# A decoder layer on one core: the recurrence's gates from exact parts, 1/rms moved into evictions, larger first transfers, and a last product in one piece

## The chip, the cores and the metric

The kernel runs on one core of a Trainium2 chip. A core has engines with queues of their own: TensorE (PE, matrix products; its weight loads are PEld), VectorE (DVE), ScalarE (ACT), GpSimd (POOL) and SyncE (SP), which here issues nearly all transfers. The metric is the device time of one execution in microseconds. One more execution is recorded by the hardware profiler, and the profile and the trace come from that one.

## The reference

The reference is one layer of a hybrid decoder in float32, for 256 tokens of 2048 features. What matters here:

```python
hn = rmsnorm(h, norm_mix_w)
q, k, v, g_ret, xr, yr, g_a, g_b = split(hn @ w_in)
q, k = rotary(q), rotary(k) * RET_QK_DIM ** -0.5
ret_out = silu(g_ret) * head_groupnorm(chunkwise_retention(q, k, v))
xr = causal_dwconv(xr, rnn_conv_w, rnn_conv_b)           # 4 taps
# rg_lru: block-diagonal gates, 16 blocks of 128 features
gate_r = sigmoid(einsum("bsgi,gij->bsgj", xb, w_a) + b_a)
gate_i = sigmoid(einsum("bsgi,gij->bsgj", xb, w_x) + b_x)
a = exp(-8 * gate_r * softplus(-lam))
u = sqrt(1 - a * a) * (gate_i * xr)
hr = scan(h_t = a_t * h_{t-1} + u_t)
merged = sigmoid(g_a) * (ret_out @ w_proj_ret) + sigmoid(g_b) * ((gelu(yr) * hr) @ w_proj_rnn)
h = h + merged @ w_mix_out
# then cross-attention over 256 memory tokens, a gated FFN (2 x 5632) with a
# 3-tap convolution, and a last rmsnorm
```

## The kernel before

**Products of exact parts.** Each float32 matrix is split into `hi`, its value rounded to the type float32r, and `lo`, the rest, so that hi + lo is exact. A large product is the sum of three products of such parts, h·hi, l·hi and h·lo (`products_n`, L314). For weights, ACT makes `hi` (L278; for the very first chunk DVE, L276) and DVE makes `lo` (L279). For the left operands `split_pair` (L394) and `split_cols` (L420) do the same. The small products inside the recurrence, `rgw` times `xr`, are the exception: they are plain float32 matmuls (L711).

**The weight stream.** All weights lie in one array, `wall`, in the order of use. A chunk is 4 k-tiles of 128 rows by 512 columns, 1 MB, that is 8 KB for each partition, and makes 24 products (2 token halves × 4 k-tiles × 3). `prefetch` (L232) loads a chunk into `raw` (3 buffers), and splits it into `hi` and `lo` (6 buffers each, two k-tiles in one), two chunks ahead of the products. `chunks` (L291) hands it to the GEMM. The first two GEMMs, q and v, are interleaved and start with smaller pieces: the first two chunks have 2 k-tiles each, and come in transfers of 2 KB for a partition; the next four in transfers of 4 KB. The left operand x, transposed (`xt`), comes two k-tiles at a time (`Pairs`, L489), in step with the weights.

**The order.** A matmul is kept in program order (`mm`, L212). The other engines' order is set by a scheduler, which takes instructions by program order and readiness; `tc.high_priority(300)` moves some ahead. `later(n, fn)` (L287) puts the call of `fn` behind the end of the chunk n+1 chunks on. So the code between GEMMs is spread over the chunks that follow. SP issues the transfers in its order, and one that waits holds up those behind it.

**1/rms of the tokens.** The first norm's weight is folded into the split of x; the factor 1/rms (`rs0`) is per token and is only known after 39 us, when x has been loaded a second time in rows and its squares summed on ACT (`sum_squares`, L462). For q and k it is put into the tables: `spread_tokens` (L447) makes two diagonal tiles of `rs0` on DVE, and PE multiplies them with ones, which spreads `rs0` over the partitions (`rsb`); `tables` (L538) multiplies sin and cos by it. For all other outputs it goes into the eviction.

**From rows to features.** A GEMM leaves tokens on partitions. `turned_rows` (L383) copies the accumulator to `rows` on DVE with high priority (L389, or L391 with the factor), ACT separates 16-bit planes (L367), two DMA transposes turn them, and one or more chunks later ACT joins them into `f` (L378), features on partitions.

**The recurrence.** It runs in four blocks b of 512 features (L735). GEMM XR of the block is turned; `conv_x` (L741) makes `xr` with ACT (L746) and DVE (L748). `RG_WAIT` = 3 chunks (and one) after that, `recur` (L704) does two of the four gate tiles at a time (`pr` = 0, 1): four float32 matmuls, eight activations on ACT (L713 to L716), and products on DVE. After the second pair follow a square root (L728), which needs another activation table, and the scan on DVE (L731), which writes to `xr`. GEMM YR of the block goes to `gelu_y` (L763), 4 chunks after it for b < 3 and 3 chunks for b = 3; it ends in two `rnn` tiles, gelu(yr) times the scan, split into parts (L401, L402). The tiles of block b are the left operand of the chunk b of w_proj_rnn (L798): `gated` (L782) runs a GEMM with O_GB first, 4 chunks, and then w_proj_rnn, 4 chunks. So block 3's tiles are needed first in the fourth chunk of the first w_proj_rnn GEMM.

**The end.** The last 512 columns of ffn_w_down (12 k-tiles here) are done by `last_down` (L986): first token half and then the second, each in two pieces of 256 columns, so that the addition of the residual and the sum of squares of one piece run under the products of the next. Each piece has an accumulator tile; `accs[0]` holds columns 0 to 255 of both token halves, `accs[1]` the others.

Tiles of 4 KB a partition come from one pool, `big`, with 27 buffers; small PSUM tiles (`sm`) have 2 buffers and accumulators (`acc`, two token halves × 512) 3.

Of the kernel before, what the change touches and what calls it, by code (L numbers as in the profile page):

```python
# [17 lines left out]
P = 128  # L18
# [17 lines left out]
FREE = 300  # L36
RG_WAIT = 3
EPS = 1e-6
# [6 lines left out]

C_ID, C_INVF, C_SIGN, C_DEC = 0, 128, 129, 130
C_WIDTH = 130 + HEADS * S


def constants():  # L50
    c = np.zeros((P, C_WIDTH), np.float32)
    c[:, C_ID : C_ID + P] = np.eye(P, dtype=np.float32)
# [85 lines left out]
def hybrid_layer(  # L138
# [45 lines left out]
    def load_rows(src, c, cs=slice(0, BW), t=None):  # L184
# [5 lines left out]
        return t  # L190

    NF2 = 2 * NF
    pa = cp.tile([P, P], F32, name="pa")
# [3 lines left out]
    cid = cp.tile([P, C_DEC], F32, name="cid")  # L197
    ident = cid[:, C_ID : C_ID + P]
    invf = cid[:, C_INVF : C_INVF + 1]
# [22 lines left out]
    def load_x(n):  # L222
        while len(xin) < n:
            t = big([P, 2, BW], s="nat")
            rows = x[0].rearrange("(t p) d -> p t d", p=P)
            c = len(xin) * BW
            sp.dma_start(out=t, in_=rows[:, :, c : c + BW])
            xin.append(t)

    at = [0]  # L230

    def prefetch(n):  # L232
        while len(ahead) < n and taken[0] < len(stream):
# [12 lines left out]
            own = early and i % 2 == 0  # L246
            cuts = range(nk + 1) if i < 2 else range(0, nk + 1, KH) if i < 6 else (0, nk)
            if own:
                xs.load(k2 + 1)
            for a, b in zip(cuts, cuts[1:]):  # L250
                sp.dma_start(out=raw[:, a:b, :], in_=src[:, a:b, :])  # L251
                if i == 0 and a == 0:
                    sp.dma_start(out=xs.rest[0], in_=xs.rest[1])  # L253
                elif own and a == 0:
                    xs.load(k2 + nk // KH)
            if i >= 6:
                load_x(min(4, 2 * i - 11))
            if i == 8:
                sp.dma_start(out=cid, in_=consts[:, 0:C_DEC])
                sp.dma_start(out=pa[:, 16:P], in_=by_feature[:, 16:P])  # L260
                sp.dma_start(out=pb, in_=by_feature[:, P : P + 80])
            if i == 13:
                sp.dma_start(out=pf.rearrange("p a n -> p (a n)"), in_=by_feature[:, P + 80 :])
            if i in (8, 9):
                for b in (2 * i - 16, 2 * i - 15):
                    sum_squares(xin[b], ss0, b, pin=True)
            parts = []
# [114 lines left out]

    def turned_rows(a, r, then, wait=1):  # L383

        rows = big([P, 2, BW], s="rows")
        with tc.high_priority(FREE):
            for tt in range(2):
                if r is None:
                    dve.tensor_copy(rows[:, tt, :], a[:, tt, :])  # L389
# [54 lines left out]

    rsb = cp.tile([P, S], F32, name="rsb")

    def spread_tokens(r):  # L447

        diag = tp.tile([P, S], F32, tag="tr", bufs=2, name=nm("diag"))
        for tt in range(2):  # L450
            dve.tensor_scalar_mul(diag[:, tt * P : (tt + 1) * P], ident, r[:, tt : tt + 1])

        def products():
            bc = small((P, S))
            for tt in range(2):
                cs = slice(tt * P, (tt + 1) * P)
                mm(bc[:, cs], ones, diag[:, cs], start=True, stop=True)
            act.copy(rsb, bc)

        return products  # L460

    def sum_squares(rows, ss, c, pin=False):  # L462

        for tt in range(2):
            junk = tp.tile([P, BW], F32, tag="tmp", name=nm("junk"))
            i = act.activation(junk, rows[:, tt, :], AF.Square, accum_out=ss[:, tt, c : c + 1])
            if pin:
                tc.keep_in_program_order(i)

# [8 lines left out]

    ss0 = sums()

# [8 lines left out]
    class Pairs(list):  # L489
# [3 lines left out]
        def load(self, n):  # L493

            while len(self.raw) < n:
                k2 = len(self.raw)
                t = tmp("xt")
                src = self.src[:, 2 * k2 : 2 * k2 + 2, :]
                if k2 == 0 and self is xs:
                    sp.dma_start(out=t[:, 0, :], in_=src[:, 0, :])  # L500
                    self.rest = (t[:, 1, :], src[:, 1, :])
                else:
                    sp.dma_start(out=t, in_=src)  # L503
                self.raw.append(t)

# [14 lines left out]
    posi = big([P, S], I32, s="posi")  # L520
    sp.dma_start(out=posi, in_=positions[0].partition_broadcast(P))

    rs0 = rstd_rows(ss0)
    spread0 = spread_tokens(rs0)
    dve.tensor_scalar_mul(half_rs0, rs0, 0.5)
# [12 lines left out]
    def tables():  # L538
        spread0()
        ang, turns, red = (tmp("rot")[:, 0, :] for _ in range(3))  # L540
# [7 lines left out]
        dve.tensor_scalar(out=red, in0=red, scalar1=3.1415925, scalar2=-3.1415925, op0=ALU.min, op1=ALU.max)  # L548
        act.activation(sin, red, AF.Sin)
        dve.scalar_tensor_tensor(out=ang, in0=red, scalar=-1.0, in1=red, op0=ALU.mult, op1=ALU.max)  # L550
        dve.tensor_scalar(out=ang, in0=ang, scalar1=-1.0, scalar2=float(np.pi / 2), op0=ALU.mult, op1=ALU.add)
        act.activation(cos, ang, AF.Sin)
        dve.scalar_tensor_tensor(out=sin, in0=sin, scalar=sign, in1=rsb, op0=ALU.mult, op1=ALU.mult)
        dve.tensor_tensor(out=cos, in0=cos, in1=rsb, op=ALU.mult)

# [147 lines left out]

    def recur(b, rgw, xr, pr, aa, tt_, ti):  # L704

        for j in (2 * pr, 2 * pr + 1):
# [28 lines left out]
    for b in range(4):  # L735
        rgw = big([P, 2, 4, P], s="rgw")
        for i, src in enumerate((rg_w_a, rg_w_x)):
            sp.dma_start(out=rgw[:, i], in_=src[0, 4 * b : 4 * b + 4].rearrange("g i j -> i g j"))
        xr = {}

        def conv_x(f, b=b, xr=xr, rgw=rgw):  # L741
            xr[0] = big([P, 4, S], s="xr")
# [9 lines left out]

            three = []

            def both(pr):
                if pr == 0:
                    three.extend(big([P, 4, S], s=n) for n in ("aa", "tt", "ti"))
                recur(b, rgw, xr[0], pr, *three)

# [47 lines left out]
    hrow = [load_rows(x, c) for c in range(4)]  # L807
    mnat = [load_rows(mem, c) for c in range(4)]
    ms = Pairs(mem_t, p_mem, 3)
# [35 lines left out]
    def memory_steps(b):  # L845
        if b == 0:
            ss = sums()
            for c in range(4):
# [137 lines left out]
    def last_down(b0, hid, n, b):  # L986
# [4 lines left out]
        accs = [acc(), acc()]  # L991
        parts = [p for _, _, ps in chunks(n, "ffn_w_down", b0 * BW, b * BW) for p in ps]
        for tt in range(2):
            last = big([P, BW + 1], s="last")
            before = sp_.tile([P, 1], F32, tag="pt3", bufs=2, name=nm("pt3"))
            for c in range(2):
                cs = slice(c * S, (c + 1) * S)
                for k in range(n):
                    hi, lo = (t[:, k % KH, cs] for t in parts[k // KH])
                    for _ in products_n(accs[c][:, tt, 0:S], hid[k // 2][:, k % 2, :], hi, lo, tt, k == 0, k == n - 1):  # L1000
                        pass
                y = last[:, c * S : (c + 1) * S + c]
                dve.tensor_add(last[:, cs], h[:, tt, cs], accs[c][:, tt, 0:S])
                junk = tp.tile([P, S + 1], F32, tag="tr", bufs=2, name=nm("junk"))
# [85 lines left out]
```

## Time and profile before

| what | value |
|---|---|
| median of 3 runs | 2006.91 us (2006.58 to 2007.68) |
| the profiled execution's own time | 2007.17 us |
| its span | 2005.4 us |
| mean granted TensorE clock | 0.999 |
| PE busy | 1995.0 us, 9012 records |
| DVE / ACT busy | 1264.9 / 1257.4 us |
| HBM read | 388.46 MB, 195 GB/s over the span |
| groups: L279 lo, DVE, 714 instructions | 859.7 us, mean 1219 ns |
| L278 hi, ACT, 712 instructions | 733.3 us, mean 1048 ns |
| L378 f, ACT, 120 instructions | 158.2 us, mean 1354 ns |
| L391 rows, DVE, 68 instructions | 47.7 us, mean 743 ns |

The span runs from the first to the last instruction; the time of the execution is 1.77 us longer. A group's mean is the duration of one instruction from start to end; where one follows another at once, they start some 0.08 to 0.10 us closer than that. In the views of the trace every row has the start in microseconds from the beginning of the span, the duration (of the whole run, where several alike follow one another), the engine and what it does; what stands in brackets is idle time just before it and what ended that. In the chain of waits each piece starts where the one before it ends. PE's matmul records for a float32 matmul come twice, so x8 there are four matmuls.

### The profile page before, as it was taken

How to read it: one execution, taken by the hardware profiler on the slowest of the kernel's cores; microseconds unless marked ns; L12 is line 12 of the kernel's file. 1: busy time of each engine (PE TensorE's matmuls, PEld its weight loads, DVE VectorE, ACT ScalarE, POOL GpSimd, SP SyncE). 2: the span in 40 equal slices, each digit the busy share in tenths (PEclk: the TensorE clock that was granted, in tenths of full speed). 3: DMA queues.
4: the chain of work that ended last, by engine and by line, in shares of the span. 5: the costliest groups of instructions: out<-in, count | busy, mean ns of one | idle time of the engine just before them, and what ended most of it. 6: DMA issues, size and time to landing. Idle time of an engine off the chain costs nothing.

```text
span 2005.4 us, 23496 instructions
## 1 busy us (share of the span) xinstructions
PE 1995.0 (99%) x9012; PEld 1660.5 (83%) x9012; DVE 1264.9 (63%) x1562; ACT 1257.4 (63%) x1508; POOL 8.8 (0%) x14
## 2 busy tenths in 40 slices
PE   9999999999999999999999999999999999999998
PEld 7888888888888888888888888888888888888887
DVE  6857756888545555466555554667774576754775
ACT  6646647988444555586676655767763577734773
POOL 0000000000000000000000000000000000000000
PEclk9999999999999999999999999999999999999999
DMA  8765757765555656787667546677775577656673
GB/s 305 243 224 164 240 197 210 220 206 184 211 192 192 202 196 215 264 273 219 216 214 215 183 169 196 223 200 230 212 229 190 179 229 221 217 201 202 207 231 126
DMA packets 191488, 423.54 MB, mean 211 GB/s; under 512 B 133776, under 2 KB 138512, under 8 KB 146320
## 3 DMA queue, kind: packets, MB, share of 16 engines
q1 hardware_dynamic: 190944, 421.52, 64.3%
q8 instruction: 70, 1.15, 0.2%
q10 hardware_dynamic: 432, 0.53, 0.1%
q14 instruction: 42, 0.34, 0.0%
HBM read 388.46 MB, written 2.10 MB: 195 GB/s over the span
## 4 chain that ended last, share of the span: by engine, by line
PE 98%; issue 0%; DMA 0%; DVE 0%; SPq 0%; ACT 0%; POOLq 0%; POOL 0%
PE acc L213 96%; PE sm L213 3%; DMA raw<-in_wall 0%; DVE lo L279 0%; SPq L251 0%; ACT nat L1024 0%; DVE rows L389 0%; ACT hi L278 0%; POOLq L1086 0%; POOL last L1012 0%; SPq L503 0%; SPq L253 0%; SPq L500 0%; POOLq L1012 0%
## 5 line engine op out<-in xcount | busy, mean ns | idle before, releaser
L213 PE MATMUL acc<-hi,s 128*128 128x512 f32 (+1 forms) x5744 | 1758.6, 388 | 0.9 <-DVE hi L276 0.9
L213 PEld LDWEIGHTS acc<-hi,s 128*128 128x128 f32 x5744 | 1073.9, 188 | 220.9 <-issue 1.6
L279 DVE TENSOR_TENSOR lo<-raw,hi 128x1024 fp32r<-128x1024 f32 (+1 forms) x714 | 859.7, 1219 | 600.3 <-ACT hi L278 579.9
L213 PE MATMUL acc<-lo,s 128*128 128x512 f32 (+1 forms) x2872 | 1112.1, 387 | 0.7 <-DVE lo L279 0.7
L278 ACT CAST hi<-raw 128x1024 fp32r<-128x1024 f32 (+1 forms) x712 | 733.3, 1048 | 490.7 <-PE acc L213 450.0
L213 PEld LDWEIGHTS acc<-lo,s 128*128 128x128 f32 x2872 | 539.2, 188 | 111.6 <-DVE lo L279 1.6
L378 ACT COPY f<-pt 128x1024 uint16<-128x1024 uint16 x120 | 158.2, 1354 | 94.7 <-DMA pt<-pl 94.7
L367 ACT COPY pl<-rows 128x1024 uint16<-128x1024 uint16 x92 | 91.6, 1043 | 41.8 <-DVE rows L391 37.5
L939 DVE SCALAR_TENSOR_TENSOR fg<-f,pf,fg 128x255 f32<-128x255 f32 (+1 forms) x88 | 37.4, 479 | 29.5 <-ACT fg L937 29.1
L391 DVE TENSOR_SCALAR rows<-acc,ro 128x512 f32<-128x512 f32 x68 | 47.7, 743 | 1.7 <-PE acc L213 1.6
L939 DVE SCALAR_TENSOR_TENSOR fv<-f,pf,fv 128x255 f32<-128x255 f32 (+1 forms) x88 | 36.1, 478 | 4.7 <-ACT fv L937 4.6
L425 DVE SCALAR_TENSOR_TENSOR s<-f,pb,s 128x256 fp32r<-128x256 f32 x48 | 20.1, 479 | 4.9 <-ACT s L424 4.9
L937 ACT ACTIVATE fg<-f,pf 128x256 f32<-128x256 f32 x44 | 22.9, 591 | 0.3
L937 ACT ACTIVATE fv<-f,pf 128x256 f32<-128x256 f32 x44 | 23.1, 591 | 0.0
L748 DVE SCALAR_TENSOR_TENSOR xr<-f,pa,xr 128x255 f32<-128x255 f32 (+2 forms) x48 | 20.2, 476 | 3.2 <-ACT xr L746 3.1
L424 ACT ACTIVATE s<-f,pb 128x256 fp32r<-128x256 f32 x48 | 20.6, 497 | 0.0
L367 ACT COPY pl<-nat 128x1024 uint16<-128x1024 uint16 x16 | 15.9, 1042 | 7.3 <-DVE nat L823 7.3
L213 PEld LDWEIGHTS sm<-s,s 128*128 128x128 f32 x144 | 18.8, 191 | 0.9
L213 PE MATMUL sm<-s,s 128*128 128x256 f32 (+1 forms) x144 | 18.6, 279 | 0.0
L957 ACT ACTIVATE ft<-fg 128x512 f32<-128x512 f32 x22 | 13.8, 629 | 7.3 <-DVE fg L939 7.3
L413 ACT ACTIVATE v<-acc,ro 128x512 fp32r<-128x512 f32 x16 | 10.9, 682 | 10.9 <-DVE v L414 10.9
L401 ACT ACTIVATE s<-fo 128x512 fp32r<-128x512 f32 x22 | 13.6, 633 | 4.1 <-DVE fo L959 4.1
(146 smaller groups left out, 578.1 us busy)
## 6 DMA issues: line engine op xcount, KB each, us to landing
raw<-in_wall SPq DMA_DIRECT2D x352, 1024.0 KB, 4.9
nat<-in_x SPq DMA_DIRECT2D x8, 512.0 KB, 8.3
raw<-in_wall SPq DMA_DIRECT2D x6, 512.0 KB, 8.1
nat<-in_mem SPq DMA_DIRECT2D x4, 512.0 KB, 8.6
xt<-in_mem_t SPq DMA_DIRECT2D x8, 256.0 KB, 5.6
pt<-pl SPq DMA_TRANSPOSE x120, 3.3
xt<-in_x_t SPq DMA_DIRECT2D x7, 256.0 KB, 8.4
out<-nat SPq DMA_DIRECT2D x6, 256.0 KB, 2.9
```

The source lines that it names most:

```text
L213: tc.keep_in_program_order(pe.matmul(*a, **k))
L278: act.copy(hi[:, ds], raw[:, cs, :])
L279: dve.tensor_tensor(out=lo[:, ds], in0=raw[:, cs, :], in1=hi[:, ds].bitcast(F32), op=ALU.subtract)
L367: act.copy(planes[:, tt], words[:, tt])
L378: act.copy(halves_[:, :, :, cs], turned_[:, :, :, cs])
L391: dve.tensor_scalar_mul(rows[:, tt, :], a[:, tt, :], r[:, tt : tt + 1])
L424: act.activation(t[:, j, 0:S], src[:, j, :], AF.Identity, scale=wcol(j))
L425: dve.scalar_tensor_tensor(out=t[:, j, S:BW], in0=src[:, j, :], scalar=wcol(j), in1=t[:, j, 0:S].bitcast(F32), op0=ALU.mult, op1=ALU.subtract,
L748: dve.scalar_tensor_tensor(out=y[:, s:S], in0=z[:, 0 : S - s], scalar=p_cw(3 - s, t), in1=y[:, s:S], op0=ALU.mult, op1=ALU.add,)
L937: act.activation(y, z[:, j, :], AF.Identity, scale=pf[:, 2, t : t + 1], bias=pf[:, 3, t : t + 1])
L939: dve.scalar_tensor_tensor(out=y[:, s:S], in0=z[:, j, 0 : S - s], scalar=pf[:, 2 - s, t : t + 1], in1=y[:, s:S], op0=ALU.mult, op1=ALU.add,)
L957: act.activation(th, gt[:, cs, :], AF.Tanh, scale=0.5)
```

## The change

1. The gates of the recurrence become three products of exact parts (`product`, L350), 256 columns wide, instead of a float32 matmul. `parts_of` makes the parts: `hi` by ACT, `lo` by DVE, as tiles of 128 × 1024 from `big`; for the gate weights 4 chunks after the block's start, for `xr` 2 chunks after `conv_x`. `RG_WAIT` goes from 3 to 4, so that both pairs of gates stand a chunk later.
2. The tables of sin and cos no longer hold 1/rms; `rsb`, `spread_tokens` and the identity in `consts` go. `turned_rows` of q and k multiplies by `rs0` (L391's form); for the first q it is not urgent any more. The sign goes into the activation of sin.
3. The first transfers: the second chunk comes in one piece of 4 KB a partition instead of two of 2 KB; `xt` from the third pair on comes in four k-tiles (4 KB); x and mem for the sums of squares come in half rows (4 KB) with one activation each, in place. The early transfers are kept in program order.
4. In `last_down`, the first token half is one product of 512 columns into `accs[0][:, 0, :]`; the second stays in two pieces, into `accs[0][:, 1, 0:256]` and `accs[1][:, 1, 0:256]`.

```diff
-RG_WAIT = 3
+RG_WAIT = 4
...
+    def load(out, in_, pin):
+        i = sp.dma_start(out=out, in_=in_)
+        if pin:
+            tc.keep_in_program_order(i)
+
+    def load_half(src, i):
+
+        t = big([P, 2 * BW], s="nat")
+        load(t, src[0, i // 2 * P : (i // 2 + 1) * P, i % 2 * 2 * BW : (i % 2 + 1) * 2 * BW], src is x)
+        return t
...
-            cuts = range(nk + 1) if i < 2 else range(0, nk + 1, KH) if i < 6 else (0, nk)
+            cuts = range(nk + 1) if i == 0 else range(0, nk + 1, KH) if i < 6 else (0, nk)
...
-    def turned_rows(a, r, then, wait=1):
+    def turned_rows(a, r, then, wait=1, urgent=True):
         rows = big([P, 2, BW], s="rows")
-        with tc.high_priority(FREE):
+        with tc.high_priority(FREE) if urgent else nullcontext():
...
+    def sum_squares(rows, ss, i):
+
+        tc.keep_in_program_order(act.activation(rows, rows, AF.Square, accum_out=ss[:, i // 2, i % 2 : i % 2 + 1]))
...
-                t = tmp("xt")
-                src = self.src[:, 2 * k2 : 2 * k2 + 2, :]
+                many = 1 if k2 < 2 else 2
+                t = big([P, 2 * many, S], s="xt")
+                src = self.src[:, 2 * k2 : 2 * (k2 + many), :]
...
-        spread0()
...
-        act.activation(sin, red, AF.Sin)
+        act.activation(sin, red, AF.Sin, scale=sign)
...
-        dve.scalar_tensor_tensor(out=sin, in0=sin, scalar=sign, in1=rsb, op0=ALU.mult, op1=ALU.mult)
-        dve.tensor_tensor(out=cos, in0=cos, in1=rsb, op=ALU.mult)
...
-            turned_rows(a, None, rotate_both, 2 - b if g + b else 3)
+            turned_rows(a, rs0, rotate_both, 2 - b if g + b else 3, g + b > 0)
...
+    def parts_of(src):
+
+        hi, lo = (big(list(src.shape), F32R, s="rp") for _ in range(2))
+        act.copy(hi, src)
+        dve.tensor_tensor(out=lo, in0=src, in1=hi.bitcast(F32), op=ALU.subtract)
+        return hi, lo
...
-                mm(gp[:, i, :], rgw[:, i, j, :], xr[:, j, :], start=True, stop=True)
+                product(
+                    gp[:, i, :], [t[:, i, j, :] for t in wparts], [t[:, j, :] for t in xparts], True, True
+                )
...
+        later(3, lambda wparts=wparts, rgw=rgw: wparts.extend(parts_of(rgw)))
...
+            three, xparts = [], []
+            later(1, lambda: xparts.extend(parts_of(xr[0])))
...
+        def total(o, tt, cs):
+            for k in range(n):
+                hi, lo = (t[:, k % KH, cs] for t in parts[k // KH])
+                for _ in products_n(o, hid[k // 2][:, k % 2, :], hi, lo, tt, k == 0, k == n - 1):
+                    pass
...
+            if tt == 0:
+                total(accs[0][:, 0, :], tt, slice(0, BW))
             for c in range(2):
                 cs = slice(c * S, (c + 1) * S)
-                for k in range(n):
-                    hi, lo = (t[:, k % KH, cs] for t in parts[k // KH])
-                    for _ in products_n(accs[c][:, tt, 0:S], hid[k // 2][:, k % 2, :], hi, lo, tt, k == 0, k == n - 1):
-                        pass
+                o = accs[c][:, 1, 0:S] if tt else accs[0][:, 0, cs]
+                if tt:
+                    total(o, tt, cs)
...
-                dve.tensor_add(last[:, cs], h[:, tt, cs], accs[c][:, tt, 0:S])
+                dve.tensor_add(last[:, cs], h[:, tt, cs], o)
```

More of the change, by code (lines that the diff above doesn't have):

```diff
@@ L1 @@
-from contextlib import ExitStack
+from contextlib import ExitStack, nullcontext
 import numpy as np
@@ L44 @@
 O_XR, O_YR, O_GA, O_GB = 6144, 8192, 10240, 12288
-C_ID, C_INVF, C_SIGN, C_DEC = 0, 128, 129, 130
-C_WIDTH = 130 + HEADS * S
+C_INVF, C_SIGN, C_DEC = 0, 1, 2
+C_WIDTH = C_DEC + HEADS * S
 def constants():
     c = np.zeros((P, C_WIDTH), np.float32)
-    c[:, C_ID : C_ID + P] = np.eye(P, dtype=np.float32)
     half = DK // 2
@@ L197, in hybrid_layer @@
     cid = cp.tile([P, C_DEC], F32, name="cid")
-    ident = cid[:, C_ID : C_ID + P]
     invf = cid[:, C_INVF : C_INVF + 1]
@@ L223, in load_x @@
         while len(xin) < n:
[L224 to L228, printed above, removed]
+            xin.append(load_half(x, len(xin)))
     at = [0]
@@ L250, in prefetch @@
             for a, b in zip(cuts, cuts[1:]):
-                sp.dma_start(out=raw[:, a:b, :], in_=src[:, a:b, :])
+                load(raw[:, a:b, :], src[:, a:b, :], early)
                 if i == 0 and a == 0:
-                    sp.dma_start(out=xs.rest[0], in_=xs.rest[1])
+                    load(*xs.rest, early)
                 elif own and a == 0:
@@ L258, in prefetch @@
             if i == 8:
-                sp.dma_start(out=cid, in_=consts[:, 0:C_DEC])
-                sp.dma_start(out=pa[:, 16:P], in_=by_feature[:, 16:P])
-                sp.dma_start(out=pb, in_=by_feature[:, P : P + 80])
+                load(cid, consts[:, 0:C_DEC], True)
+                load(pa[:, 16:P], by_feature[:, 16:P], True)
+                load(pb, by_feature[:, P : P + 80], True)
             if i == 13:
-                sp.dma_start(out=pf.rearrange("p a n -> p (a n)"), in_=by_feature[:, P + 80 :])
+                load(pf.rearrange("p a n -> p (a n)"), by_feature[:, P + 80 :], True)
             if i in (8, 9):
                 for b in (2 * i - 16, 2 * i - 15):
-                    sum_squares(xin[b], ss0, b, pin=True)
+                    sum_squares(xin[b], ss0, b)
             parts = []
@@ L442, in hybrid_layer @@
     p_xa, p_mem, p_ffn = (col(pb, b) for b in (32, 48, 64))
[L445 to L468, printed above, removed]
+    def sum_squares(rows, ss, i):
+        tc.keep_in_program_order(act.activation(rows, rows, AF.Square, accum_out=ss[:, i // 2, i % 2 : i % 2 + 1]))
     def sums():
@@ L477, in rstd_rows @@
         return rsqrt_small(var, 2, 1.0 / D, EPS)
-    ss0 = sums()
+    ss0 = sums()[:, :, 0:2]
     def rsqrt_small(ap, n, scale, eps):
@@ L496, in load @@
                 k2 = len(self.raw)
-                t = tmp("xt")
-                src = self.src[:, 2 * k2 : 2 * k2 + 2, :]
+                many = 1 if k2 < 2 else 2
+                t = big([P, 2 * many, S], s="xt")
+                src = self.src[:, 2 * k2 : 2 * (k2 + many), :]
                 if k2 == 0 and self is xs:
-                    sp.dma_start(out=t[:, 0, :], in_=src[:, 0, :])
+                    load(t[:, 0, :], src[:, 0, :], True)
                     self.rest = (t[:, 1, :], src[:, 1, :])
                 else:
-                    sp.dma_start(out=t, in_=src)
-                self.raw.append(t)
+                    load(t, src, self is xs)
+                self.raw += [t[:, 2 * i : 2 * i + 2, :] for i in range(many)]
         def __getitem__(self, i):
@@ L520, in hybrid_layer @@
     posi = big([P, S], I32, s="posi")
-    sp.dma_start(out=posi, in_=positions[0].partition_broadcast(P))
+    load(posi, positions[0].partition_broadcast(P), True)
     rs0 = rstd_rows(ss0)
-    spread0 = spread_tokens(rs0)
     dve.tensor_scalar_mul(half_rs0, rs0, 0.5)
@@ L702, in hybrid_layer, with recur @@
     rnn = []
-    def recur(b, rgw, xr, pr, aa, tt_, ti):
+    def parts_of(src):
[3 more added lines that the diff above has]
+        return hi, lo
+    def recur(b, wparts, xparts, xr, pr, aa, tt_, ti):
         for j in (2 * pr, 2 * pr + 1):
@@ L738, in hybrid_layer, with conv_x @@
             sp.dma_start(out=rgw[:, i], in_=src[0, 4 * b : 4 * b + 4].rearrange("g i j -> i g j"))
-        xr = {}
-        def conv_x(f, b=b, xr=xr, rgw=rgw):
+        xr, wparts = {}, []
+        later(3, lambda wparts=wparts, rgw=rgw: wparts.extend(parts_of(rgw)))
+        def conv_x(f, b=b, xr=xr, wparts=wparts):
             xr[0] = big([P, 4, S], s="xr")
@@ L751, in conv_x @@
                     )
-            three = []
+            three, xparts = [], []
+            later(1, lambda: xparts.extend(parts_of(xr[0])))
             def both(pr):
@@ L757, in both @@
                     three.extend(big([P, 4, S], s=n) for n in ("aa", "tt", "ti"))
-                recur(b, rgw, xr[0], pr, *three)
+                recur(b, wparts, xparts, xr[0], pr, *three)
             for pr in range(2):
@@ L807, in hybrid_layer @@
     hrow = [load_rows(x, c) for c in range(4)]
-    mnat = [load_rows(mem, c) for c in range(4)]
+    mnat = [load_half(mem, i) for i in range(4)]
     ms = Pairs(mem_t, p_mem, 3)
@@ L846, in memory_steps @@
         if b == 0:
-            ss = sums()
+            ss = sums()[:, :, 0:2]
             for c in range(4):
```

## The prediction

> **What bounds the kernel now.** I read the busy times and the chain of waits first.
>
> ```profile
> PE 1995.0 (99%) x9012; PEld 1660.5 (83%) x9012; DVE 1264.9 (63%) x1562; ACT 1257.4 (63%) x1508; POOL 8.8 (0%) x14
> ...
> PE 98%; issue 0%; DMA 0%; DVE 0%; SPq 0%; ACT 0%; POOLq 0%; POOL 0%
> ```
>
> PE is the chain from 13 us to 1991 us. So a PE microsecond saved is a microsecond of span, and work added on ACT or DVE is free until PE has to wait for it. The pieces of the chain in order of time (start, us, what) give PE's prices:
>
> ```profile
> 4.02 6.79 DMA raw<-in_wall
> 10.81 0.02 issue
> 10.84 1.06 ACT hi L278
> ...
> 45.74 1.29 DVE rows L389 x2
> 47.03 1.14 DVE lo L279
> ...
> 481.25 5.45 PE acc L213 x24
> 486.70 1.73 PE sm L213 x8
> 488.43 484.17 PE acc L213 x2136
> 972.60 2.87 PE sm L213 x24
> 975.48 43.55 PE acc L213 x192
> ```
>
> A product with 512 columns costs 43.55/192 = 0.2268; with 256 columns 2.87/24 = 0.1196; four float32 gate matmuls (8 records) 1.73, so 0.4325 each. A chunk of 24 products lasts 5.45. Outside the head the only breaks in PE are one at 48 and the tail.
>
> Whether ACT and DVE have room is not read from 63% but from the recurrence. Busy time there, two stretches (stretch, length, then PE, PEld, DVE, ACT):
>
> ```profile
> 398.00:425.00 27.00, 27.00 (x121) 22.36 (x120) 25.11 (x36) 26.54 (x32) 0.00 (x0) 1.00 0.65 213
> 480.00:491.00 11.00, 11.00 (x50) 9.23 (x49) 6.15 (x8) 10.96 (x20) 0.00 (x0) 1.00 0.59 232
> ```
>
> ACT is full at the very place where the change gives it more; DVE is at 93% in the first. The clock column is 1.00, so PE's prices hold.
>
> **The change part by part.** The sum is made against the profiled execution, 2007.17 (span 2005.4 and 1.77 around it), 0.26 above the median of 2006.91; the differences are then put on the median.
>
> *Gates on PE.* 32 float32 matmuls go: 32 × 0.4325 = 13.84. 96 products of 256 columns come: 96 × 0.1196 = 11.48. **−2.36**.
>
> *1/rms in the evictions.* The diagonal's two matmuls go (0.36, from 45.54 to 45.91), and with them the wait at 48.22, where PE wants a lo that DVE does after the urgent pair of rows (the 1.29 above). From 45.32 to 48.56 there are 10 products: 3.24 against 10 × 0.2268 = 2.27, so **−0.97**. The rows now need rs0, which POOL finishes at 39.0, well before 45.7. sin and cos lose two DVE multiplies, a product wait nobody has; nothing on the path.
>
> *4 KB pieces.* The head's waits of PE:
>
> ```profile
> 5.24 1.42 PE L213 MATMUL acc<-hi,s 128*128 128x512 f32 x4 [0.41 <-DVE hi L276]
> ...
> 7.59 1.17 PE L213 MATMUL acc<-hi,s 128*128 128x512 f32 x4 [0.48 <-DVE hi L276]
> ...
> 13.20 0.50 PE L213 MATMUL acc<-lo,s 128*128 128x512 f32 x1 [0.53 <-DVE lo L279]
> ```
>
> In all PE loses about 2.0 here (0.98 around 7.6, 0.24 at 11.9, 0.80 at 13.2, with the refill after each). Throughput is about 320 GB/s from 7 to 10 us, where 2 KB pieces land, and about 420 from 10 to 16. The second chunk's raw, 0.52 MB, would save 0.39 us at the better rate, and SP issues one transfer fewer (0.47) ahead of the next. Against that its first casts wait for all 4 KB rather than for 2 KB. I take **−0.3**; bounds −1.0 (both later waits gone) and +0.5 (one cast's length later). In the Trainium skill, DMA: Bandwidth & Descriptors, section "Why small descriptors are slow (HBM only)", joining descriptors is worth it only up to 256 B each; by that, 2 KB to 4 KB gives 0 instead of −0.3. The two rates here speak for a gain, but other transfers are mixed in, and the difference is within my bounds.
>
> *Squares* of x (and mem) now take one activation of 128x1024 a load, about the 1.06 of the square root's row, instead of two of 128x512 of 0.62 each with a read of 0.18: less ACT work before 39 us, off the path. The order of x and xt on SP's queue moves (xt in 4 k-tiles, after the raw it used to precede); PE has no wait between 14 and 45 that this could lengthen by the rows, so 0, held by the ±0.5 above.
>
> *The last piece.* The first tokens' 72 products of 256 columns (17.27/144 = 0.1199 each in that stretch, 8.63) become 36 of 512 (8.16): −0.47. But the two half accumulators become one tile, and the second tokens' first product uses it too: it waits for both additions that read the first tokens' result.
>
> ```profile
> 1984.79 0.42 DVE L1003 TENSOR_TENSOR last<-nat,acc 128x256 f32<-128x256 f32 x1
> ```
>
> PE's last product ends 0.39 after issue; then two additions (0.42 and 0.34 in line), with 0.04 to pass each semaphore: about 1.2 less the 0.23 that PE would have spent anyway, 1.0 to 1.1. Net **+0.6**; if the wait isn't there, −0.47.
>
> *ACT and DVE in the recurrence, where I see the loss.* Per block of 512 features come two splits into parts (of the gate weights and of xr): on ACT 2 casts of 128x1024 like L278's (1.05), on DVE 2 subtractions like L279's (1.22), so 8.4 and 9.8 us in all. And the gates stand a chunk later. I went along the changed program's queues with the durations of the rows above, letting each instruction start when its engine and its operands are ready; the same walk on the old program gives PE one wait in this kernel's middle, 0.37 at 45, as the trace has it (0.39).
>
> Block 3 decides. Its rnn tiles are the left operand of w_proj_rnn's fourth chunk. Before, after the second pair of gates:
>
> ```profile
> 488.14 0.48 ACT L713 ACTIVATE tr<-sm,h 128x256 f32<-128x256 f32 x1
> ...
> 492.21 1.28 ACT L728 ACT_TABLE_LOAD   x1
> 493.50 1.06 ACT L728 ACTIVATE tt<-tt 128x1024 f32<-128x1024 f32 x1
> 494.58 1.28 ACT L770 ACT_TABLE_LOAD   x1
> ...
> 501.45 0.62 ACT L401 ACTIVATE s<-rn 128x512 fp32r<-128x512 f32 x1
> ```
>
> From the activations to the first split of rnn 13.3 us pass, with two casts of weights (L278) between. The gates (486.70) stand before O_GB's fourth chunk, w_proj_rnn starts at 493.88 and wants the tile at 493.88 + 3 × 5.45 = 510.2: it is there at 502, 8 us early.
>
> After, the gates stand right ahead of w_proj_rnn; call its start T. Two casts of weights stand on ACT between the two pairs' activations, so it comes to the second pair at T+1.7 instead of T−0.7. Then, in its queue: 8 activations 3.42, both f copies of YR (formerly before the gates) 2.43, table load 1.28, square root 0.97, square 0.52, table load 1.28, two sig 1.17, a cast 1.05, a wait of 0.8 for DVE's y2 (behind the scans), tanh 0.54, square 0.52, four casts 3.8, tanh 0.54, a cast 0.95, and the split 0.63 (start to start where the next follows at once): 19.9, ready at T+21.6 where PE wants it at T+16.35. **5.25**, then 0.87 for its lo on DVE (L407 behind a weight's lo), 0.98 for the second tile: **+7.1**. Bounds: if ACT comes to it at once, 2.4 less, and with DVE's wait of 0.8 gone too, about +4; with ACT and DVE each 3% longer over these 21 us (0.65 each) about +8.5. What is queued behind are the weights' casts of the next chunks, which then have two chunks of lead to catch up, so nothing more follows.
>
> Blocks 0 to 2: in block 0 DVE works without a break for 9 us (gate tail, rgw's subtraction, rows, ti, four scans) ahead of a weight's lo that YR's GEMM wants: 1.16. In block 1 the first gates wait for the lo of xr, behind conv_x's subtraction chain and two weights' lo: 0.96; block 2 0.26 there, and 1.2 for a weight's lo behind the scans. **+3.6**, bounds 0 (DVE 4% quicker and all fit) and +6 (transfers landing later).
>
> Sum: −2.36 − 0.97 − 0.3 + 0.6 + 7.1 + 3.6 = +7.7; 2007.17 + 7.7 = 2014.9, on the median **2014.6**.
>
> **The rivals.**
>
> *Not slower: the split comes in time.* If ACT's order is looser than I read it (PE's buffers release casts later, so that the split overtakes them in time) and DVE fits, only PE's terms stay: −2.36 − 0.97 − 0.3 + 0.6 = −3.0, 2003.9; without the wait in the last piece −4.1, 2002.8. It decides where the chain after the gates is under 17 us instead of 19.9. For it: DVE has 37% idle in the span and PE no wait here before. Against: ACT's 10.96 of 11.00. Chance 0.16, 0.07 of it faster.
>
> *Only block 3, at its lower bound:* −3.0 + 4 = +1.0, 2007.9 (up to 2010 with one wait of the other blocks). Chance 0.11.
>
> *The lag grows:* a cast late on ACT frees raw buffers late, so SP's transfers and the transposes behind them start late: block 3 8.5, the others 6 and 2 for the transfers, 2020. For it: the DMA queue is one, in order, and the engines carry up to 0.8 in the stretches of 480 us. Chance 0.10.
>
> *Table loads hold ACT longer than their row.* In the rows above the load takes 1.28 and the next activation starts within 0.01 of its end. Should a load cost its own length again where ACT's queue is dense, block 3's two add 2 × 1.28 = 2.6: 2017.2. The rows show no such gap, so 0.03. The Trainium skill, ScalarE: Activation LUTs, section "What ACT_TABLE_LOAD costs", has 1.38 us of drain behind each load; by it the two would add 2.8.
>
> *It doesn't do what it says:* if the products of exact parts ran at the float32 price, 96 × 0.4325/2 = 20.8 instead of 11.5, +9.3 more, 2024. The 256-column row of exact parts (0.1196) excludes it nearly: 0.01.
>
> **How the numbers follow.** The forecast keeps 0.59; its own range, from the sensitivity of the two recurrence terms (ACT and DVE ±3%), is 2011 to 2018.5. To hold 8 in 10 the range reaches down to the second rival and up to part of the third: 2006.5 to 2019.5; outside are the first rival (0.16) and some of the third. A measurement of this kernel tells 0.2%, 4.0 us, from no change. Faster (under 2002.9): 0.07. Same (to 2010.9): 0.09 of the first rival, 0.11 of the second, 0.02 of the forecast's lower edge, 0.22. Slower: 0.71.
>
> **What would show it.** Right: PE waits of 4 to 8 us in the fourth chunk of the first w_proj_rnn GEMM (near 510 us), released by ACT's split L406; small ones by DVE near 361, 388 and 461; 12 records per pair of gates with 1.44 instead of 1.73; no break at 48; one of about 1 us between the two tokens' halves in the end. Wrong: PE unbroken through 360 to 515, or waits there whose releaser is a transfer; head waits that grow.

## The result and the profile after

| | before | changed |
|---|---|---|
| median of 5 runs | 2007.17 us | 2022.85 us |
| range | 2006.58 to 2007.68 | 2020.76 to 2024.91 |
| profiled span | 2005.4 us | 2021.0 us |
| mean granted TensorE clock | 0.999 | 0.996 |

The changed kernel is slower by 0.8%: ratio 1.0079, 95% interval 1.0068 to 1.0090. The forecast had the side and the place, and about half of the size: +7.7 forecast, +15.7 measured, above the range's 2019.5. The executions also lie further apart, 4.2 us instead of 1.1.

The busy times and the chain of waits of the changed kernel:

```profile
PE 1998.0 (99%) x9004; PEld 1660.0 (82%) x9004; DVE 1272.0 (63%) x1566; ACT 1263.0 (62%) x1499; POOL 8.8 (0%) x14
...
PE 93%; ACT 3%; DVE 2%; DMA 1%; issue 1%; SPq 0%; POOLq 0%; POOL 0%; DVEq 0%; ACTq 0%
```

PE's share of the chain went from 98% to 93%, ACT and DVE came in with 5%. PE is busy for 3 us more than before, although its products take less time: some ran slower. The pieces of the chain (start, us, what), the few that matter:

```profile
366.47 1.13 DVE lo L284
367.64 27.02 PE acc L222 x112
394.66 1.43 PE sm L222 x12
...
469.52 1.15 DVE lo L284
...
470.71 20.26 PE acc L222 x88
...
521.98 0.70 DVE s L407
...
522.72 464.71 PE acc L222 x2039
987.44 2.87 PE sm L222 x24
```

The same last row stood at 972.60 before. So at 987.44 all but 0.8 us of the loss is made, and from 522.72 on PE is unbroken again up to the last piece. The gates show their gain, 1.43 for 12 products where the four float32 matmuls took 1.73. PE's waits by what ended them (us in total, times, longest); these are idle times, and the distances between PE's starts, from which the waits are counted further down, give somewhat more for each:

```profile
PE acc L222 <- DVE lo L284: 5.2, 3, 2.7
PE acc L222 <- ACT s L406: 4.6, 1, 4.6
PE acc L222 <- ACT hi L283: 1.1, 1, 1.1
...
PE sm L222 <- DVE rp L689: 1.0, 1, 1.0
PE acc L222 <- DVE hi L281: 0.9, 1, 0.9
PE acc L222 <- DVE last L1003: 0.8, 1, 0.8
...
```

Every one of these but the head's (L281) is new. What follows the larger ones is seen in the busy time by stretches (stretch, length, then busy time of PE, PEld, DVE, ACT, POOL; granted clock; DMA):

```profile
364.00:368.00 4.00, 1.21 (x4) 0.66 (x4) 3.56 (x5) 4.00 (x5) 0.00 (x0) 0.88 0.69 131
368.00:372.00 4.00, 4.00 (x13) 3.18 (x13) 3.42 (x5) 3.98 (x6) 0.00 (x0) 0.69 0.70 262
372.00:376.00 4.00, 4.00 (x19) 3.29 (x19) 3.97 (x6) 3.99 (x5) 0.00 (x0) 1.00 0.84 289
...
520.00:524.00 4.00, 2.08 (x4) 1.38 (x5) 4.00 (x6) 2.19 (x4) 0.00 (x0) 0.58 0.68 244
524.00:528.00 4.00, 4.00 (x11) 3.06 (x11) 2.14 (x3) 0.00 (x0) 0.00 (x0) 0.56 0.71 252
528.00:532.00 4.00, 4.00 (x19) 3.29 (x18) 1.97 (x2) 2.10 (x2) 0.00 (x0) 1.00 0.57 240
```

From 368 to 372 and from 524 to 528 PE is busy all the time, but these rows have 13 and 11 products where the row behind each has 19: the granted clock is 0.69 and 0.56. A product took 0.427 there, start to start, instead of 0.2268. ACT is busy for the whole 4.00 us of the first row.

The account, from the distances between PE's starts in the trace (what exceeds a product's own time):

| part | forecast | measured |
|---|---|---|
| gates' products | −2.36 | −2.4 (8 × 0.30) |
| wait and diagonal at 46 to 48 | −0.97 | −0.94 |
| head | −0.3 | −0.7 here, none on average (below) |
| blocks 0 to 2, waits | +3.6 (1.16, 0.96, 1.46) | +8.9 (4.4, 1.6, 2.9) |
| block 3, waits | +7.1 | +5.7 |
| products at half clock (behind block 0's waits and behind block 3's) | 0 | +3.8 (1.4 and 2.4) |
| last piece | +0.6 | +0.8 |

These make +15.2 of the span's +15.6.

### The profile page after: what moved, and what is told of

Its sections match the earlier page's. It is cut to its first block, busy times and chain, and to the rows that moved or that the text cites. A ratio compares the mean times of both kernels' runs of the same rounds, so it can differ in the third digit from the quotient of the medians.

```text
span 2021.0 us, 23470 instructions
## 1 busy us (share of the span) xinstructions
PE 1998.0 (99%) x9004; PEld 1660.0 (82%) x9004; DVE 1272.0 (63%) x1566; ACT 1263.0 (62%) x1499; POOL 8.8 (0%) x14
## 4 chain that ended last, share of the span: by engine, by line
PE 93%; ACT 3%; DVE 2%; DMA 1%; issue 1%; SPq 0%; POOLq 0%; POOL 0%; DVEq 0%; ACTq 0%
PE acc L222 91%; PE sm L222 2%; ACT f L383 1%; ACT hi L283 0%; DVE lo L284 0%; DMA raw<-in_wall 0%; DVE xr L721 0%; ACT pl L372 0%; ACT aa L705 0%; ACT tt L706 0%; DVE xr L739 0%; DMA xt<-in_x_t 0%; ACT tr L703 0%; DVE ti L719 0%; ACT ti L704 0%
## 5 line engine op out<-in xcount | busy, mean ns | idle before, releaser
L222 PE MATMUL acc<-hi,s 128*128 128x512 f32 x5720 | 1758.8, 389 | 7.8 <-ACT s L406 4.6
L222 PE MATMUL acc<-lo,s 128*128 128x512 f32 x2860 | 1112.0, 389 | 5.3 <-DVE lo L284 5.2
L396 DVE TENSOR_SCALAR rows<-acc,ro 128x512 f32<-128x512 f32 x76 | 53.4, 744 | 4.7 <-PE acc L222 4.7
```

Of the source, the lines that this page charges most:

```text
L222: tc.keep_in_program_order(pe.matmul(*a, **k))
```

## The experiments

Theory A: the loss is the gate part's alone (a later chain for block 3, more work on ACT and DVE where they are full, and a lower clock behind PE's waits). Rival B: the splits' work makes it, the delay is harmless. Rival C: other parts of the change delay the recurrence. "Three" and "four" chunks below are RG_WAIT.

### 1. Float32 gates, three chunks

```diff
-RG_WAIT = 4
+RG_WAIT = 3
...
-                product(
-                    gp[:, i, :], [t[:, i, j, :] for t in wparts], [t[:, j, :] for t in xparts], True, True
-                )
+                mm(gp[:, i, :], wparts[0][:, i, j, :], xr[:, j, :], start=True, stop=True)
...
-        later(3, lambda wparts=wparts, rgw=rgw: wparts.extend(parts_of(rgw)))
+        wparts.append(rgw)
...
-            later(1, lambda: xparts.extend(parts_of(xr[0])))
```

> The changed kernel with the whole gate part undone: float32 gates again, three chunks later, no splits into parts. All else of the change stays. Theory A (the loss is made by the gate part alone: a later chain for block 3, more work on ACT and DVE, and the lower clock after PE's waits): PE has no wait in the recurrence, so what is left is the head's gain of 1.6 and the tail's loss of 0.8: about 2006.3. Rival C (the other parts, xt in the common pool and the rows without priority, delay the recurrence): waits of several us stay near 360 to 520, 2012 or more.

2007.05 us (ratio to before 0.9999, 0.9989 to 1.0008), 0.75 above what was expected. No wait of PE in the recurrence. Rival C is out: the rest of the change neither delays the recurrence nor brings anything that can be told from nothing.

### 2. Float32 gates, four chunks

The edit is that of the first experiment without the line of RG_WAIT.

> The changed kernel with float32 gates, but still four chunks later. Theory A: block 3's chain is still late, by about 4 us at the fourth chunk of the first w_proj_rnn GEMM, and some us of half clock follow; no waits in blocks 0 to 2: 2010 to 2014. Rival B (the splits' work alone makes the loss, the delay is harmless): no wait, about 2006.

2014.45 us (1.0039, 1.0024 to 1.0054), 0.45 above the expected range. In its trace PE waits 1.75 and 1.45 (by distances between starts) for block 3's first tile, once for ACT's part of it and once for DVE's (PE's timeline; the bracket is idle time before the row):

```profile
513.47 0.49 PE L222 MATMUL acc<-hi,s 128*128 128x512 f32 x1 [1.59 <-ACT s L406]
515.15 0.50 PE L222 MATMUL acc<-hi,s 128*128 128x512 f32 x1 [1.18 <-DVE s L407]
```

Then it runs some products at half clock. Blocks 0 to 2 have small waits too, 0.9 the longest, which theory A had not expected. The delay alone costs 7.4 us: rival B is out as the only cause.

### 3. Exact parts, three chunks

```diff
-RG_WAIT = 4
+RG_WAIT = 3
```

> The changed kernel with the exact parts, but the gates only three chunks later. Theory A: block 3's chain comes a chunk (5.45 us) earlier, so its wait falls to 2 us or less; the gates of block 1 now stand closer to the split of xr and wait about 4 us for it (cast and subtraction); 2008 to 2014. Rival B: as slow as the changed kernel, 2020 or more.

2013.97 us (1.0035, 1.0022 to 1.0048). The waits stand where they were expected, at the first gates of block 1 (PE's timeline):

```profile
385.93 0.38 PE L222 MATMUL sm<-rp,rp 128*128 128x256 f32 x1 [1.66 <-ACT rp L688]
388.20 2.21 PE L222 MATMUL sm<-rp,rp 128*128 128x256 f32 x11 [1.89 <-DVE rp L689]
```

PE first waits for the cast of xr (L688), does one product, and waits for the subtraction (L689); 3.41 us at half clock follow. So the chunk of delay was there to hide the splits; it moves the cost to block 3. The four kernels together:

| median, us | three chunks | four chunks |
|---|---|---|
| float32 gates | 2007.05 | 2014.45 |
| exact parts | 2013.97 | 2022.85 |

Delay +7.4 and parts +6.9 add to 14.3; both together cost 15.8. Each makes waits on PE by itself. That the sum nearly comes out does not make the two independent, for the waits are others: block 1's first gates wait 4.0 with parts and three chunks, and 1.0 in the changed kernel; block 0's waits are 1.3 with the delay alone, none with the parts alone, and 4.4 with both.

### 4 and 8. Artificial waits

At twelve places of the kernel before, all after 1350 us, PE was made to wait for a chain of n tiny POOL operations:

```diff
+    def probe(n):
+        a, b = small(), small()
+        t = big([P, P], s="probe")
+        mm(a[:, 0, 0:P], ones, ones, start=True, stop=True)
+        dve.tensor_copy(t, a[:, 0, 0:P])
+        for _ in range(n):
+            pool.tensor_tensor(out=t[:, 0:1], in0=t[:, 0:1], in1=mhalf[:, 0:1], op=ALU.pow)
+        mm(b[:, 0, 0:P], ones, t, start=True, stop=True)
```

In the fourth, n is 3, 5, 7 or 10. In the eighth, n is 0, 1 or 2, or 1 twice, and eight small products stand behind each wait.

> The kernel before, with twelve artificial waits of PE in the cross-attention and FFN, 8 chunks apart: a small product, a copy, a chain of 3, 5, 7 or 10 tiny POOL operations of about 0.55 each, a small product that needs its end; each length three times. Theory A (PE runs at half clock for some us after it has stood for longer than about 3.5 us): waits of about 2 and 3 us cost only their own length; those of about 4.5 and 6 us are followed by products at 0.43 instead of 0.227 for 3.4 or 6.8 us. Rival (the half clock in the changed kernel comes from something else than the wait's length): products at 0.227 behind all of them, or 0.43 behind the short ones too.

> The kernel before with twelve shorter artificial waits: chains of 0, 1 and 2 tiny POOL operations, about 1.5, 2.5 and 3.2 us of standstill, and one pair of waits of 2.5 us with 2 us of products between them; each three times. Theory A (a standstill counts by how much of a stretch of 3.4 us it fills): no half clock behind the first kind, none or seldom behind the second, some behind the third, and some behind the pair. Rival (only one unbroken wait of 3.4 us or more counts): never behind the pair, nor behind the third kind.

The waits, as distances between PE's starts: 1.1 us (three times), 2.7 (three), 3.3 (three), pairs of 2.7 and 1.3 to 1.6 (three); 3.9 (three), 5.1 to 9 (nine; a POOL operation took longer than supposed). Half clock followed none of the 1.1 and of the single 2.7, one of the three pairs, and all from 3.3 up. In that pair it began at 1702.42, before the second wait at 1703.83: the first wait of 2.7 did it alone, so one of six waits of 2.7 did. The fourth experiment has no wait under 3.9, so its rival's case, half clock behind short ones, is tested by the eighth alone. Both expectations had the direction right, and the rival of the eighth, that only an unbroken 3.4 us counts, is out.

The trace also records when the granted clock changes. All changes of one execution lie on one grid of 3.413 us, and half clock lasts for 3.41, 6.83 or 10.24, that is one to three such stretches. Three pairs of stretches on that grid in the eighth experiment, and under them one of the fifth, which follows below (columns as above; each pair is a stretch with a wait and the one behind it):

```profile
1402.05:1405.46 3.41, 1.74 (x15) 1.74 (x16) 1.57 (x3) 3.38 (x5) 1.44 (x1) 1.00 0.80 300
1405.46:1408.87 3.41, 3.41 (x19) 2.88 (x19) 3.37 (x9) 1.71 (x4) 0.00 (x0) 1.00 0.64 262
1449.83:1453.24 3.41, 0.45 (x4) 0.45 (x5) 1.88 (x3) 3.38 (x4) 1.98 (x2) 1.00 1.08 418
1453.24:1456.65 3.41, 3.41 (x18) 3.41 (x17) 3.08 (x8) 2.36 (x5) 0.00 (x0) 0.50 0.70 284
...
1699.00:1702.42 3.42, 1.48 (x13) 1.48 (x14) 1.49 (x3) 3.39 (x5) 1.43 (x1) 1.00 0.78 304
1702.42:1705.83 3.41, 2.24 (x12) 1.94 (x11) 1.50 (x5) 1.34 (x3) 0.64 (x1) 0.50 0.96 370
...
363.46:366.88 3.42, 1.82 (x6) 0.97 (x6) 3.38 (x6) 3.42 (x4) 0.00 (x0) 1.00 0.41 77
366.88:370.29 3.41, 1.77 (x5) 1.38 (x5) 2.39 (x3) 3.41 (x5) 0.00 (x0) 0.50 0.63 118
```

The reader is to compare PE's busy time in the first row of a pair with the clock in the second: in the eighth 1.74 busy and 1.00; 0.45 busy and 0.50; 1.48 busy and 0.50. The fifth's pair, 1.82 busy and 0.50, shows that busy time, in which the ends of products are modelled, is not fine enough. Counted by the distances between PE's starts, less each product's own time, all stretches fall in order: of those that began at full clock, from 60 us to the last piece in the twelve profiles, at most 1.84 us of standstill left the clock alone, and 1.94 us or more always halved it for the next stretch. How the slower first product behind a wait is counted moves single stretches by 0.1 to 0.2 (the fifth's has 2.04 with it and 1.83 without), so the border is near 1.9 and not known closer. Waits within one stretch add up: before 367.07 in the changed kernel lie 1.31 and 1.25, neither enough alone, and the clock was halved. By this count standstill under about 1.8 us in all can't do it, one wait of 2.7 does it only where the grid leaves enough of it in one stretch, and a standstill of more than twice 1.94 must.

### 5. O_GB's second GEMM first

```diff
+    i = plan.index(("w_proj_rnn", 0, NT, 0))
+    plan[i : i + 2] = plan[i + 1], plan[i]
...
+    two = [sigmoid2(O_GB, b) for b in range(2)] + [None] * 2
-    mb = [gated(O_GB, "w_proj_rnn", rnn, b, big([P, 2, BW], s="mb")) for b in range(4)]
+    mb = [gated(O_GB, "w_proj_rnn", rnn, b, big([P, 2, BW], s="mb"), two[b]) for b in range(4)]
```

`sigmoid2` is the first half of `gated`, the GEMM and its two activations.

> The changed kernel with one thing moved: O_GB's second GEMM stands ahead of the first w_proj_rnn GEMM, so that block 3's tiles are wanted 4 chunks (21.8 us) later. Theory A (block 3's wait and the half clock behind it are one of the two main losses): PE's wait of 4.9 near 520 and the 3 us at half clock go, blocks 0 to 2 keep theirs: 2014 to 2016. Rival (ACT and DVE are full, and the lost time only turns up one GEMM later): 2019 or more.

2017.23 us (1.0053, 1.0040 to 1.0065): 5.6 less than the changed kernel, and 1.2 above the expected range. Block 3's wait is gone and no wait follows up to the last piece, so the rival falls. But in the profiled execution block 2's wait of 2.5 us fell into one stretch of the grid (2.42 us of standstill) and halved the clock, where in the changed kernel's profile the grid cut the same wait into 1.59 and 1.35 and the clock stayed; and block 0's was followed by 6.83 us at half clock instead of 3.41.

### 6. The last piece's tiles swapped (on the first experiment's kernel)

```diff
-                o = accs[c][:, 1, 0:S] if tt else accs[0][:, 0, cs]
+                o = accs[1 - c][:, 1, 0:S] if tt else accs[0][:, 0, cs]
```

> The kernel of the first experiment (float32 gates, three chunks) with the last piece's accumulators swapped: the second tokens' first piece goes to the tile that the first tokens do not use. Theory A (the second tokens' first product waits for the two additions because it shares a tile with them, 1.0 us): the gap of 1.23 between the products goes to 0.23, and the end comes 1 us earlier: 2006.0. Rival (the gap is the additions' own, whatever the tile): 2007.0.

2006.25 us (0.9994, 0.9985 to 1.0003), 0.8 below the first experiment's. PE's distance of 1.233 at the first tokens' end in the first experiment, the same in the changed kernel, is gone from the trace. The row behind it, in the changed kernel:

```profile
2004.28 0.50 PE L222 MATMUL acc<-hi,s 128*128 128x256 f32 x2 [0.84 <-DVE last L1003]
```

The median agrees; the times alone could not have shown 1 us.

### 7. All three losses treated

The edits of 3, 5 and 6, and xr split by pairs of gates:

```diff
-            later(1, lambda: xparts.extend(parts_of(xr[0])))
+            later(1, lambda: xparts.extend(parts_of(xr[0][:, 2 * i : 2 * i + 2, :]) for i in range(2)))
...
-                    gp[:, i, :], [t[:, i, j, :] for t in wparts], [t[:, j, :] for t in xparts], True, True
+                    gp[:, i, :], [t[:, i, j, :] for t in wparts], [t[:, j % 2, :] for t in xparts[pr]], True, True
```

> Exact parts kept, and all three losses treated: gates three chunks later, xr split in two halves so that the first pair of gates waits for half of it, O_GB's second GEMM ahead of the first w_proj_rnn, the last piece's tiles swapped. Theory A: PE's waits in the recurrence 1 to 3 us in all, no half clock; against the kernel of the sixth experiment -2.4 for the gates and +1 to +3 for the waits: 2004.5 to 2007. Rival B (the splits' work makes waits wherever the gates stand): 2010 or more.

2004.77 us (ratio to before 0.9987, 0.9978 to 0.9996): 2.3 us faster than before and 18 faster than the changed kernel. Against the sixth experiment's kernel, with float32 gates and the old order of GEMMs, it is 1.5 faster, where the gates' products alone are worth 2.4. One wait of PE is left from 60 us to the last piece (PE's timeline), and the clock is never halved in between:

```profile
392.49 0.98 PE L224 MATMUL sm<-rp,rp 128*128 128x256 f32 x6 [0.36 <-ACT ti L706]
```

### 9 and 10. The seventh without halves, and with four chunks

In 9, xr is split whole again. In 10, RG_WAIT is 4 again.

> The kernel of the seventh experiment with xr split whole again, as the change does it. Theory A (with the gates three chunks after conv_x, block 1's first gates wait for the whole of xr's cast and subtraction): two waits near 386 of together 3.6 us as in the third experiment, with 1.0 us of half clock behind them, and nothing else: about 2009.5. Rival (the moved O_GB GEMM and the last piece alone made the seventh fast): about 2005.

> The kernel of the seventh experiment with the gates four chunks after conv_x, as the change has them. Theory A (the delay alone costs, because block 0's and block 2's scans then stand ahead of a weight's lo on DVE, and casts ahead of the activations on ACT): waits near 365 and 470 come back, 4 to 8 us with half clock in some executions: 2009 to 2013. Rival (with block 3 hidden and xr in halves, the chunk of delay is harmless): about 2005.

9: 2010.39 us (1.0019, 1.0009 to 1.0028). The waits are the third experiment's, 2.38 and 1.89 of idle time at block 1's first gates, this time with 6.83 us at half clock. 10: 2011.9 us (1.0023, 1.0014 to 1.0033), with 0.83 and 1.62 near 366 and half clock behind them; the wait near 470 that was expected did not come, one of 1.28 at 496, before gates of block 3, did. So each of the two edits is needed: halves are worth 5.6 us, the third chunk 7.1.

## Why the prediction fell short, point by point

**The bound.** PE is the chain, and ACT and DVE have no room in the recurrence: right, and the ground of all that came.

**The gates on PE, −2.36:** right, 1.43 for a pair.

**1/rms in the evictions, −0.97:** right. None of the nine kernels with this part waits between 20 and 60 us.

**4 KB pieces, −0.3:** not seen. The first scores start at 144.46, 144.35 and 143.80 in the three profiles with the old head, on average 144.20. With the new one they start at 142.81 to 144.39, on average 143.72 in nine. These starts come 0.48 earlier, of which the part before should make 0.94; so the new head costs 0.5, within a scatter of about 1 us. The changed kernel's own profile, with 142.81, was the luckiest of the nine, so the −0.7 of the account is luck. The head was changed in several ways at once, and no run takes the pieces of 4 KB alone. The rule weighed against the rows (the Trainium skill, DMA: Bandwidth & Descriptors, section "Why small descriptors are slow (HBM only)": joining is worth it only up to 256 B) came nearer than the two rates.

**The last piece, +0.6:** right, 1.233 less 0.227 for the wait; the sixth experiment removed it.

**Block 3, +7.1:** right in place and mechanism; the size was 5.7, and the 1.4 too much hid a part of what was missed elsewhere. The chain ran as it was laid out. ACT's timeline of the changed kernel:

```profile
501.73 0.47 ACT L703 ACTIVATE tr<-sm,h 128x256 f32<-128x256 f32 x1
...
505.14 2.56 ACT L383 COPY f<-pt 128x1024 uint16<-128x1024 uint16 x2
507.72 1.28 ACT L718 ACT_TABLE_LOAD   x1
509.01 1.06 ACT L718 ACTIVATE tt<-tt 128x1024 f32<-128x1024 f32 x1
...
515.69 3.87 ACT L283 CAST hi<-raw 128x1024 fp32r<-128x1024 f32 x4
...
520.93 0.63 ACT L406 ACTIVATE s<-rn 128x512 fp32r<-128x512 f32 x1
```

From 501.73 to the split's end at 521.56 are 19.8 us (19.9 forecast). The copies, the table load and the four casts stand where the queue had them. ACT came to it 0.5 sooner after the gates than supposed, and the second tile, forecast to cost 0.98, was in time. The load's next activation starts 0.01 behind its end, so the rival of dearer table loads is out. So is, for this kernel, the drain of 1.38 us that the Trainium skill, ScalarE: Activation LUTs, section "What ACT_TABLE_LOAD costs", adds to each load.

**Blocks 0 to 2, +3.6 with +6 as its bound: mis-sized, 8.9 measured; this step failed.** Block 0 carries most: 4.4 instead of 1.16. In block 0 the chain of waits leaves PE for a transfer, and ACT stands for it ahead of the first gate activations (one row of the chain and ACT's timeline of the changed kernel, then the same place of ACT's timeline before the change):

```profile
336.27 8.07 DMA raw<-in_wall
...
344.44 2.00 ACT L283 CAST hi<-raw 128x1024 fp32r<-128x1024 f32 x2 [6.64 <-DMA raw<-in_wall]
346.34 0.47 ACT L703 ACTIVATE tr<-sm,h 128x256 f32<-128x256 f32 x1
```

```profile
338.21 1.99 ACT L278 CAST hi<-raw 128x1024 fp32r<-128x1024 f32 x2 [1.77 <-DMA raw<-in_wall]
340.11 0.47 ACT L713 ACTIVATE tr<-sm,h 128x256 f32<-128x256 f32 x1
```

The raw for these two casts was issued behind two gate-weight transfers and two transposes and took 8.07 us to land, where the usual is 4.9. ACT came to the activations at 346.34, though the gates' first products started at 342.16. Before, the transfer behind the gate weights took 8.20 too, but the activations stood ahead of its casts; with the gates a chunk later they stand behind them. The difference from 4.9, about 3 us, is what block 0's wait grew by. But the transfer alone does not make it: with float32 gates (experiment 2) it took 8.20, ACT stood for 7.17, and block 0's waits were only 1.3; in experiment 10 it took 5.75, and they were 3.0. With three chunks (3, 7, 9) they were 0.4 at most. So the chunk of delay and the splits are both needed, which runs show; how much of the 4.4 is the transfer's was not tried by itself. Block 2's 2.9 instead of 1.46 is one wait for a weight's lo behind the scans, as the forecast had it; why it is twice as long stays open. The rival of a growing lag, given 0.10, came nearest with its late transfers.

**"The clock column is 1.00, so PE's prices hold": this step failed too.** Before, the clock stood at 1.00 in a stage where PE never stopped. The forecast put new waits into the kernel and kept the price of a product. Behind 4.4 us of waits within 6 us in block 0 and behind block 3's wait PE ran at 0.427 a product, 3.8 us in all in the profiled execution, more or less in others: experiments 4 and 8 show the rule. The Trainium skill, TensorE: Matmul & The Clock Gate, section "Part 1: The HAM clock gate (the "warmup" mystery)", has a free-running window of 3413 ns; the traces agree in length (3.413) and in that its phase differs from profile to profile. It puts the lower clock behind an idle window; here one that stood still for 1.94 of 3.41 us was enough.

**The range** left out both: its upper edge was made from longer waits, at full speed. Of the 15.2 in the table, 5.3 more than forecast come from blocks 0 to 2 and 3.8 from the clock, 1.4 less from block 3.

## What to carry to other kernels

Where PE never stops, ask for every edit what is late next on the engines that feed it, by going along their queues instruction by instruction; a busy share of 63% over the span says nothing of a stage that stands at 98%. A wait of PE has two prices, its own length and, once standstill fills more than about half of one 3.4 us stretch, the half speed of the next stretch; here standstill under 1.8 us in a stretch never had it. A cheaper product that needs parts made by full engines paid here only once the parts came in small pieces, the gates stood a chunk earlier and the result was wanted a GEMM later: with the last piece's tiles swapped too, that turned +15.7 us into −2.3.

## What was not expected of the hardware

Half clock is decided stretch by stretch on a grid that does not start with the kernel: at most 1.84 us of standstill in 3.413 had no effect, 1.94 always had, with a border not known closer than 0.1 or 0.2. So one and the same wait costs nothing more, or 1.7 us more for each full stretch at half clock behind it, by where the grid cuts it. A grid that falls otherwise in each execution fits the changed kernel's 4.2 us between its executions: the shortest, 2020.76, has a mean granted clock of 0.998, the longest, 2024.91, of 0.995. Ten executions of the seventh experiment's kernel, which has no such wait, lie within 1.0 (2004.00 to 2004.97; an eleventh took 7870.85). But it is not all of the scatter: the sixth's eleven, without a wait in the recurrence and all at 0.999, lie 3.0 apart.
